# Which PSUM banks plain tiles, norm sums and the last mixer products use, and the order of the first down pair, in a fused FFN–mixer–FFN step

## The chip, the core and the metric

The kernel runs on one core of a Trainium2 chip. A core has five engines that work side by side and meet through semaphores: TensorE (PE; its weight loads are shown as PEld), VectorE (DVE), ScalarE (ACT), GpSimd (POOL) and SyncE (SP, which here only issues DMAs). TensorE writes its results into PSUM, eight banks of 512 fp32 values in each of 128 partitions; VectorE and ScalarE read them from there. The metric is the time of one execution in microseconds, and the median of several is compared.

## The reference

One step of a hybrid decoder trunk on 520 tokens (a prompt of 512 and 8 single tokens that go on from a state), model width 1024, FFN width 2816, all in fp32:

```python
h = h + 0.5 * swiglu(rms_norm(h, ffn1_norm), ffn1_w_gate, ffn1_w_up, ffn1_w_down)
m, ... = hybrid_mixer(rms_norm(h, mix_norm), ...)   # in-projection, pooling, conv, SSD scan, gate, out-projection
h = h + m
h = h + 0.5 * swiglu(rms_norm(h, ffn2_norm), ffn2_w_gate, ffn2_w_up, ffn2_w_down)
return rms_norm(h, final_norm), new pool, conv and ssm states
# swiglu(x, wg, wu, wd) = (silu(x @ wg) * (x @ wu)) @ wd
```

## The kernel before

Activations lie feature by token: 128 features on the partitions, 520 tokens along the free dimension, worked on as two halves of 260 (`HALVES`, `HB`). A product in fp32 is made from parts: each operand is split into a high part (fp32r) and the rest (`split`: ScalarE rounds the high part into `whi` or `shi`, VectorE subtracts for `wlo` or `slo`), and `mm3` (L121 to L126) issues three matmuls, high by high (L122), high by low (L125) and low by high (L126).

**FFN.** The 22 tiles of the FFN width are taken in chunks of 6, 6, 6 and 4. A gate tile and its up tile, by the two halves of the input features, make a 2 by 2 block product, which is done with seven smaller products instead of eight (`product`, p = 1 to 7). One of the sums, in the trace `A`, takes one PSUM bank, and the other two, `BE`, take a pair. The weights of the seven products are the raw ones (`whi_4a`, `whi_4b` for tile 4) and sums of them that VectorE builds (L346 to L348, then split into `shi_4c`/`slo_4c` and `shi_4d`/`slo_4d`). In between ScalarE copies a sum aside (`ac`, L380) before the next product adds to it. `gates` and `close` (L392 to L415) put the sums together, multiply by the norm's factor `r_f`, take Silu and multiply gate and up. The order for a tile is in `step`: close the tile before, then products 5, 6, 3, 7, 2; product 4 comes after the next tile's first one.

Before the first chunk is in its stride, some tiles are done another way: `plain` takes the unsplit fp32 weights (one matmul of two passes for each, L311), and `plain_out` (L314 to L325) reads them: L319 multiplies the gate half by `r_f`, L321 is Silu, L322 multiplies by `r_f` again, L324 multiplies by the up half. In FFN1 these are tiles 0 and 3, in FFN2 tile 0. `rstds` computes the norm's factor: a matmul with ones into a bank (`psr`, L168), Sqrt and reciprocal (L169, L170).

After each of the first three chunks come its down products, two output tiles at a time (`(c, 0)`, `(c, 2)`, `(c, 4)`, `(c, 6)`: names `A1d`, `BE1d` in FFN1 and `A2d`, `BE2d` in FFN2), again by seven products. Their activations are the outputs of pairs of tiles, sums and differences of which `g_split` builds and splits: `gx` and `go` are the first and second tile of a pair, `xd` (in the trace `gd`) the differences, `gt` the split parts (L264 high, L265 low). The last chunk's down (`down`, L462, in FFN1) is made tile by tile (`dn`): two tiles are begun with three of the four FFN tiles, as the last one's output comes late, and are then completed one after the other; VectorE adds each half to `h` (L478), and `after` makes the mixer's input from it.

**Mixer.** Stages in an order written by hand (plan strings) do the in-projection (`dt`, `inbc`, `inx`, `inz`), pooling, convolution, SSD scan, gate and out-projection (`wout`, three units; the last has `fin`, which makes FFN2's input from `h`). FFN2's tile 0 (`plain`) is laid between the last out-projection products by the plan `"h0 h2 h1 n0 h3 n1 n2 n3"`.

**PSUM in the FFNs** is one pool with three tags, two buffers each: `A` (one bank), `BE` (two banks) and `ps` (one bank): 2 + 4 + 2 banks. A tile that takes a buffer over waits until the readers of the one before are done. `bank(name)` gives a `ps` bank.

**What sets the order.** The program is written in order, and a scheduler then chooses each engine's instruction order by a simulation of its timeline; each engine runs its list in that order. `keep_in_program_order` (argument `pin` of `mm3`) holds an instruction at its place in the program's order; `high_priority` moves work ahead. So another buffer or pin can change the order of other engines' work too.

Of the kernel before, what the change touches and what calls it, by code (L numbers as in the profile page):

```python
# [61 lines left out]
def tile_trunk_step(ctx: ExitStack, tc: tile.TileContext, ins: dict, outs: dict):  # L62
# [9 lines left out]
    dr = ctx.enter_context(tc.tile_pool(name="dr", bufs=1, space=DRAM))  # L72
    ps = [None]

    def bank(name):
        return ps[0].tile([P, 512], F32, tag="ps", name=name)

    vx = act.tile([P, NVEC + KD * NT], F32, tag="h", name="h")
    vec = vx[:, :NVEC]
# [48 lines left out]
    def ws(w, k, m=P):  # L128
        return w[:, k * m : (k + 1) * m]
# [32 lines left out]
        nc.scalar.activation(out=sq, in_=h[:, d], func=AF.Square)  # L162
        nc.vector.tensor_tensor(out=nx[2], in0=nx[2], in1=sq, op=ALU.add)

    def rstd(r, acc, hs, width, name):
        ps = bank(f"psr_{name}")[:, : hs.stop - hs.start]
        for k, sq in enumerate(acc):
            nc.tensor.matmul(ps, ones, sq, start=k == 0, stop=k == len(acc) - 1)  # L168
        nc.scalar.activation(out=r[:, hs], in_=ps, func=AF.Sqrt, bias=eps, scale=1.0 / width)  # L169
        nc.vector.reciprocal(out=r[:, hs], in_=r[:, hs])  # L170

    def rstds(nx, name):
        for b, hs in enumerate(HALVES):
            rstd(nx[3], [nx[2][:, hs]], hs, D, f"{name}{b}")

# [28 lines left out]
    class Ffn:  # L204
# [42 lines left out]
        def g_split(self, f, late=None):  # L247
            role = self.role(f)
            if role == "plain" and late is not False:
                self.g_plain(f, self.out[f])  # L250
            if role != "second":
                return
            last = f == self.chunks[self.chunk[f]][-1]
            if not last and late is False:
                return
            gx, go = self.gx, self.out[f]
            if not last or late is not True:
                self.gt[f] = (self.gp.tile([P, 14, HB], F32R, tag="gt", bufs=3, name=f"gt{self.i}_{f}"),
                              self.gp.tile([P, 4, HB], F32, tag="xd", name=f"gd{self.i}_{f}"))
            t, xd = self.gt[f]  # L260

            def low(x, q):
                hi, lo = t[:, 0:7][:, q], t[:, 7:14][:, q]
                nc.scalar.copy(hi, x)  # L264
                nc.vector.tensor_tensor(out=lo, in0=x, in1=hi.bitcast(F32), op=ALU.subtract)  # L265

            if not last or late is not True:
                nc.vector.tensor_tensor(out=xd[:, 0], in0=gx[:, 0], in1=gx[:, 1], op=ALU.subtract)
                nc.vector.tensor_tensor(out=xd[:, 1], in0=go[:, 1], in1=gx[:, 1], op=ALU.subtract)
                nc.vector.scalar_tensor_tensor(out=xd[:, 2], in0=xd[:, 1], scalar=-1.0, in1=gx[:, 0], op0=ALU.mult,  # L270
                                               op1=ALU.subtract)
                low(gx[:, 0], 0)
                if last:
                    low(go[:, 1], 2)
                    low(xd[:, 0:3], slice(3, 6))
            if last and late is False:
                return
            nc.vector.scalar_tensor_tensor(out=xd[:, 3], in0=xd[:, 2], scalar=-1.0, in1=go[:, 0], op0=ALU.mult,
                                           op1=ALU.subtract)
            if last:  # L280
                low(go[:, 0], 1)
                low(xd[:, 3], 6)
            else:
                low(go, slice(1, 3))
                low(xd, slice(3, 7))
# [11 lines left out]
                nc.sync.dma_start(out=next(q), in_=next(q))  # L297

        def plain(self, f, xg, j, us=(0, 1)):
            for u in us:  # L300
                if (f, u) not in self.banks:
                    n = f"P{self.i}_{f}{u}"
                    if f and u == 0:
                        bs = [ps[0].tile([P, 512], F32, tag="A", bufs=2, name=f"{n}{b}") for b in range(2)]
                    else:
                        t = ps[0].tile([P, 2, 512], F32, tag="BE", bufs=2, name=n)
                        bs = [t[:, 0], t[:, 1]]
                    self.banks[f, u] = bs
                for q in range(2):
                    for b, slot in enumerate(((0, 1), (3, 2))):  # L310
                        nc.tensor.matmul(self.banks[f, u][b][:, :HB], ws(self.raw[f][:, u], j + 4 * q), xg[:, slot[q]],  # L311
                                         start=j == q == 0, stop=j == 3 and q == 1, skip_group_check=True)
# [42 lines left out]
        def product(self, k, p):  # L355
# [13 lines left out]
            for j in range(n):  # L369
                if isinstance(k, tuple):  # L370
                    t = self.gt[self.chunks[k[0]][2 * j + 1]][0]
                    xhi, xlo = t[:, slot], t[:, 7 + slot]
                else:
                    xhi, xlo = xth[:, j, slot], xtl[:, j, slot]
                mm3(out[:, :HB], ws(whi, k0 + j), ws(wlo, k0 + j), xhi, xlo, opens and j == 0,
                    j == n - 1, skip_group_check=True)
            a, c = self.ac[k]
            keep = {1: a[:, 0], 6: a[:, 1], 7: c[:, 0], 5: c[:, 1]}.get(p)
            if keep is not None:
# [82 lines left out]
        def down(self, c, lo, hi, after):  # L462
            n = hi - lo
            banks, units = {}, {}

            def part(d, ks):
                if d not in units:
                    units[d] = load_unit(ins[f"w{self.i}d"][d, :, lo * P : hi * P], n * P, f"{self.i}d{d}_{c}")
                    banks[d] = ps[0].tile([P, 2, 512], F32, tag="BE", bufs=2, name=f"dn{self.i}_{d}_{c}")
                wh, wl = units[d]  # L470
                for b in range(2):
                    for k in ks:
                        g = self.g[lo + k]
                        mm3(banks[d][:, b, :HB], ws(wh, k), ws(wl, k), g[:, 0, b], g[:, 1, b], k == 0, k == n - 1)

            def done(d):
                for b, hs in enumerate(HALVES):
                    nc.vector.tensor_tensor(out=h[:, d, hs], in0=banks[d][:, b, :HB], in1=h[:, d, hs], op=ALU.add)  # L478
# [12 lines left out]
        def down_by_half(self, c, lo, after, wd):  # L491
# [186 lines left out]
def mixer(tc, ins, outs, e):  # L678
# [556 lines left out]
```

## Time and profile before

| | us |
|---|---|
| median of 3 runs | 984.54 (983.57 to 985.28) |
| the profiled execution, as a whole | 984.47 |
| its span (what the trace covers) | 982.6 |
| PE busy in the span | 951.5 |
| DVE busy | 877.8 |
| ACT busy | 678.2 |

FFN1 runs from the start to about 361 us, the mixer to about 633, FFN2 to the end. In the views that follow, a timeline row gives start, duration (both us), engine, line, operation, output<-inputs, shape, the number of instructions that the row holds, and in brackets the engine's idle time before it and what ended it. A row of stages gives the stretch and its length, then for PE, PEld, DVE, ACT and POOL the busy time and the number of instructions, and last the granted TensorE clock, the DMA engines' busy share and GB/s. A row of waits gives engine, line and what was waited for, then the total, the count and the longest. Tile names in rows are without buffer numbers, except those of weights (`whi_1d_0a`: down weights, first pair, part a).

### The profile page before, as it was taken

The page shows a single profiled execution, that of the slowest core. Times are in us where ns is not written, and L with a number is a line of the kernel's source. Part 1 is how long each engine was busy: PE and PEld are TensorE (multiplying, and loading weights), DVE is VectorE, ACT ScalarE, POOL GpSimd, SP SyncE. Part 2 cuts the span into 40 slices and gives each one's busy share as a digit, 9 for nine tenths or more (in the row PEclk, how much of TensorE's full clock was granted, in tenths as well). Part 3 has the DMA queues.
Part 4 walks back from the last instruction along what each step waited for, and adds up shares of the span by engine and source line. Part 5 has one row for each costly group of instructions (what it writes and reads, how often), then busy time and mean ns, then how long its engine had stood idle before and what let it go on. Part 6 is the DMA issues. An engine that isn't in the chain of part 4 may idle for free.

```text
span 982.6 us, 20242 instructions
## 1 busy us (share of the span) xinstructions
PE 951.5 (97%) x7636; PEld 927.4 (94%) x7636; DVE 877.8 (89%) x1624; ACT 678.2 (69%) x1263; POOL 217.9 (22%) x319
## 2 busy tenths in 40 slices
PE   7999999999999999999999999999999999999995
PEld 6899999999999999999899998989999999999995
DVE  7899899989989698788979987999999999999976
ACT  7677677677777475685754335678788888888864
POOL 0112211121121000157411000113333233233300
PEclk9999999999999999999999999999999999999998
DMA  5565766576566243262335232456687768767732
GB/s 182 161 172 114 191 161 143 133 186 175 124 149 165 65 148 119 87 210 86 115 120 165 96 115 90 106 152 164 164 213 185 183 156 223 190 155 189 190 91 88
DMA packets 63571, 145.46 MB, mean 148 GB/s; under 512 B 9257, under 2 KB 22505, under 8 KB 63473
## 3 DMA queue, kind: packets, MB, share of 16 engines
q1 hardware_dynamic: 41168, 103.78, 33.2%
q0 software_dynamic: 22304, 40.38, 22.5%
q8 instruction: 60, 0.98, 0.4%
q14 instruction: 39, 0.31, 0.1%
HBM read 136.80 MB, written 7.34 MB: 147 GB/s over the span
## 4 chain that ended last, share of the span: by engine, by line
PE 85%; DVE 8%; ACT 3%; issue 2%; DMA 1%; POOL 1%; SPq 0%; DVEq 0%; ACTq 0%
PE A L126 7%; PE A L122 7%; PE A L125 7%; PE BE L122 6%; PE BE L125 6%; PE BE L126 6%; PE P L311 3%; PE wo L122 2%; PE wo L125 2%; PE wo L126 2%; PE inz L122 2%; PE A2d L125 2%; PE A2d L126 2%; PE A1d L125 2%; PE A1d L126 2%
## 5 line engine op out<-in xcount | busy, mean ns | idle before, releaser
L380 ACT COPY ac<-A 128x260 f32<-128x260 f32 x123 | 45.1, 369 | 16.8 <-PE A L126 16.5
L311 PE MATMUL P<-xg_f,raw 128*128 128x260 f32 x192 | 45.9, 398 | 5.5 <-DMA raw<-in_w1gu 5.5
L346 DVE TENSOR_TENSOR s<-raw 128x1024 f32<-128x1024 f32 x41 | 49.8, 1216 | 1.4 <-DMA raw<-in_w2gu 1.4
L311 PEld LDWEIGHTS P<-xg_f,raw 128*128 128x128 f32 x192 | 37.5, 199 | 11.5 <-ACT xg_f L188 5.4
L943 POOL DMA_DIRECT2D out_nss<-hs x32 | 20.6, 643 | 79.2 <-DVE hs L961 74.0
L106 ACT CAST whi_wo<-raw_wo 128x1024 fp32r<-128x1024 f32 x12 | 12.5, 1046 | 36.5 <-issue 9.2
L125 PE MATMUL wo<-catg,whi_wo 128*128 128x260 f32 x128 | 36.4, 285 | 1.3 <-DVE catg L1092 1.3
L122 PE MATMUL wo<-catg,whi_wo 128*128 128x260 f32 x128 | 37.3, 292 | 0.3 <-DVE h L1061 0.3
L122 PE MATMUL inz<-xh_mx,whi_inz 128*128 128x260 f32 x128 | 36.8, 288 | 0.0
L122 PE MATMUL inx<-xh_mx,whi_inx 128*128 128x260 f32 x128 | 36.4, 285 | 0.0
L126 PE MATMUL wo<-catg,wlo_wo 128*128 128x260 f32 x128 | 36.3, 284 | 0.0
L126 PE MATMUL inz<-xh_mx,wlo_inz 128*128 128x260 f32 x128 | 36.2, 283 | 0.0
L126 PE MATMUL inx<-xh_mx,wlo_inx 128*128 128x260 f32 x128 | 36.2, 283 | 0.0
L125 PE MATMUL inz<-xl_mx,whi_inz 128*128 128x260 f32 x128 | 36.2, 283 | 0.0
L125 PE MATMUL inx<-xl_mx,whi_inx 128*128 128x260 f32 x128 | 36.1, 282 | 0.0
L392 DVE TENSOR_TENSOR tg<-BE,ac 128x520 f32<-128x520 f32 x41 | 28.3, 691 | 5.2 <-PE BE L126 5.2
L807 DVE SCALAR_TENSOR_TENSOR A<-U,h,A 128x544 f32<-128x544 f32 x36 | 28.0, 778 | 4.3 <-ACT A L805 3.3
L401 DVE TENSOR_TENSOR tg<-tg,r_f 128x520 f32<-128x520 f32 x41 | 28.4, 694 | 1.3 <-ACT tg L399 1.0
L398 DVE TENSOR_TENSOR tg<-tg,r_f 128x520 f32<-128x520 f32 x41 | 28.4, 692 | 0.1
L347 DVE TENSOR_TENSOR s<-s,raw 128x512 f32<-128x512 f32 x41 | 28.0, 682 | 0.0
L348 DVE TENSOR_TENSOR s<-s,raw 128x512 f32<-128x512 f32 x41 | 27.9, 681 | 0.0
L399 ACT ACTIVATE tg<-tg 128x520 f32<-128x520 f32 x41 | 26.1, 637 | 1.0 <-DVE tg L398 0.9
(1787 smaller groups left out, 4747.4 us busy)
## 6 DMA issues: line engine op xcount, KB each, us to landing
raw<-in_w2gu SPq DMA_DIRECT2D x44, 512.0 KB, 4.9
raw<-in_w1gu SPq DMA_DIRECT2D x42, 512.0 KB, 4.7
raw_1d<-in_w1d SPq DMA_DIRECT2D x24, 384.0 KB, 4.0
raw_2d<-in_w2d SPq DMA_DIRECT2D x24, 384.0 KB, 4.0
raw_wo<-in_w_out SPq DMA_DIRECT2D x12, 512.0 KB, 4.8
ab<-scr_acs SPq DMA_DIRECT2D x8, 512.0 KB, 4.4
h<-in_state_ssm SPq DMA_DIRECT2D x16, 256.0 KB, 3.8
raw_inz<-in_w_in SPq DMA_DIRECT2D x8, 512.0 KB, 4.1
```

The lines of the kernel that those rows point to most:

```text
L122: first = nc.tensor.matmul(ps, whi, xhi, start=start, stop=False, **kw)
L125: nc.tensor.matmul(ps, whi, xlo, start=False, stop=False, **kw)
L126: nc.tensor.matmul(ps, wlo, xhi, start=False, stop=stop, **kw)
L311: nc.tensor.matmul(self.banks[f, u][b][:, :HB], ws(self.raw[f][:, u], j + 4 * q), xg[:, slot[q]], start=j == q == 0, stop=j == 3 and q == ...
L346: nc.vector.tensor_tensor(out=s1, in0=diag, in1=up0, op=ALU.add)
L347: nc.vector.tensor_tensor(out=s2[:, 0], in0=s1[:, 1], in1=raw[:, 0, :nb], op=ALU.add)
L348: nc.vector.tensor_tensor(out=s2[:, 1], in0=s2[:, 0], in1=raw[:, 0, nb : 2 * nb], op=ALU.add)
L380: nc.scalar.copy(keep, out[:, :HB])
L392: nc.vector.tensor_tensor(out=tg, in0=self.BE[k][:, :, :HB], in1=a, op=ALU.add)
L398: nc.vector.tensor_tensor(out=tg, in0=tg, in1=r, op=ALU.mult)
L401: nc.vector.tensor_tensor(out=tg, in0=tg, in1=r, op=ALU.mult)
L807: nc.vector.scalar_tensor_tensor(out=A[:, :n], in0=U[:, j : j + n], scalar=w(j), in1=A[:, :n], op0=ALU.mult, op1=ALU.add)
```

## The change

1. `bank` takes a tag. The up half (u = 1) of every plain tile goes into the two `ps` banks and the gate half into a `BE` pair. Before, tile 0 had both halves in `BE` pairs, and tile 3 its gate half in the two `A` banks and its up half in a `BE` pair.
2. The norm sums of the FFNs (`scales`) use `A` banks instead of `ps`.
3. The last out-projection products (`wout` with `fin`) use `A` banks instead of `ps`.
4. In `g_split` of a chunk's last pair the low parts of the differences `xd[:, 0:3]` are written ahead of those of `go[:, 1]`.
5. In the first down pair of a chunk (`(c, 0)`), the first matmul of each product is held in program order.
6. FFN1's last down begins three tiles with three of four FFN tiles instead of two; the third has its sums in the two `ps` banks.

```diff
-    def bank(name):
-        return ps[0].tile([P, 512], F32, tag="ps", name=name)
+    def bank(name, tag="ps"):
+        return ps[0].tile([P, 512], F32, tag=tag, name=name)
...
-    def rstd(r, acc, hs, width, name):
-        ps = bank(f"psr_{name}")[:, : hs.stop - hs.start]
+    def rstd(r, acc, hs, width, name, tag="ps"):
+        ps = bank(f"psr_{name}", tag)[:, : hs.stop - hs.start]
...
-    def rstds(nx, name):
+    def rstds(nx, name, tag="ps"):
         for b, hs in enumerate(HALVES):
-            rstd(nx[3], [nx[2][:, hs]], hs, D, f"{name}{b}")
+            rstd(nx[3], [nx[2][:, hs]], hs, D, f"{name}{b}", tag)
...
                 low(gx[:, 0], 0)
                 if last:
+                    low(xd[:, 0:3], slice(3, 6))
                     low(go[:, 1], 2)
-                    low(xd[:, 0:3], slice(3, 6))
...
         def plain(self, f, xg, j, us=(0, 1)):
-            for u in us:
+            for u in sorted(us, reverse=True):
                 if (f, u) not in self.banks:
                     n = f"P{self.i}_{f}{u}"
-                    if f and u == 0:
-                        bs = [ps[0].tile([P, 512], F32, tag="A", bufs=2, name=f"{n}{b}") for b in range(2)]
+                    if u:
+                        bs = [bank(f"{n}{b}") for b in range(2)]
                     else:
                         t = ps[0].tile([P, 2, 512], F32, tag="BE", bufs=2, name=n)
                         bs = [t[:, 0], t[:, 1]]
                     self.banks[f, u] = bs
+            for u in us:
...
                 mm3(out[:, :HB], ws(whi, k0 + j), ws(wlo, k0 + j), xhi, xlo, opens and j == 0,
-                    j == n - 1, skip_group_check=True)
+                    j == n - 1, pin=j == 0 and isinstance(k, tuple) and k[1] == 0, skip_group_check=True)
...
         def scales(self):
-            rstds(self.nx, f"f{self.i}")
+            rstds(self.nx, f"f{self.i}", "A")
...
-                    banks[d] = ps[0].tile([P, 2, 512], F32, tag="BE", bufs=2, name=f"dn{self.i}_{d}_{c}")
+                    if d == 2:
+                        banks[d] = [bank(f"dn{self.i}_{d}_{c}{b}") for b in range(2)]
+                    else:
+                        t = ps[0].tile([P, 2, 512], F32, tag="BE", bufs=2, name=f"dn{self.i}_{d}_{c}")
+                        banks[d] = [t[:, 0], t[:, 1]]
...
-            part(0, range(n - 1))
-            part(1, range(n - 1))
-            part(0, range(n - 1, n))
-            done(0)
-            part(1, range(n - 1, n))
-            done(1)
-            for d in range(2, KD):
-                part(d, range(n))
+            for d in range(3):
+                part(d, range(n - 1))
+            for d in range(KD):
+                part(d, range(n - 1, n) if d < 3 else range(n))
                 done(d)
...
-                ps = bank(f"wo{j}_{d}{b}")
+                ps = bank(f"wo{j}_{d}{b}", "ps" if fin is None else "A")
```

More of the change, by code (lines that the diff above doesn't have):

```diff
@@ L473, in part @@
                         g = self.g[lo + k]
-                        mm3(banks[d][:, b, :HB], ws(wh, k), ws(wl, k), g[:, 0, b], g[:, 1, b], k == 0, k == n - 1)
+                        mm3(banks[d][b][:, :HB], ws(wh, k), ws(wl, k), g[:, 0, b], g[:, 1, b], k == 0, k == n - 1)
             def done(d):
                 for b, hs in enumerate(HALVES):
-                    nc.vector.tensor_tensor(out=h[:, d, hs], in0=banks[d][:, b, :HB], in1=h[:, d, hs], op=ALU.add)
+                    nc.vector.tensor_tensor(out=h[:, d, hs], in0=banks[d][b][:, :HB], in1=h[:, d, hs], op=ALU.add)
                     after(d, b, hs)
-            part(0, range(n - 1))
-            part(1, range(n - 1))
-            part(0, range(n - 1, n))
-            done(0)
-            part(1, range(n - 1, n))
-            done(1)
-            for d in range(2, KD):
-                part(d, range(n))
+            for d in range(3):
+                part(d, range(n - 1))
+            for d in range(KD):
+                part(d, range(n - 1, n) if d < 3 else range(n))
                 done(d)
```

## The prediction

> **What bounds the kernel now.** I read the page's busy shares and chain first, then the busy time by stage, then the list of what TensorE waited for, then the timeline round each wait that the change can touch.
>
> ```profile
> PE 951.5 (97%) x7636; PEld 927.4 (94%) x7636; DVE 877.8 (89%) x1624; ACT 678.2 (69%) x1263; POOL 217.9 (22%) x319
> PE 85%; DVE 8%; ACT 3%; issue 2%; DMA 1%; POOL 1%; SPq 0%; DVEq 0%; ACTq 0%
> ```
>
> TensorE is busy for 951.5 of 982.6 us, so only 31.1 us of idle are there for any reordering to win, and VectorE (DVE) at 89% is the next in line. By stage (length, busy PE, PEld, DVE, ACT, POOL):
>
> ```profile
> 61.00:340.00 279.00, 276.60 (x2289) 274.92 (x2287) 251.79 (x412) 196.20 (x347) 49.53 (x59) 1.00 0.62 148
> 340.00:368.00 28.00, 26.25 (x212) 25.28 (x213) 24.91 (x58) 20.30 (x44) 0.70 (x2) 1.00 0.38 130
> 600.00:661.00 61.00, 58.56 (x423) 55.60 (x422) 52.37 (x81) 41.98 (x69) 7.98 (x11) 1.00 0.42 115
> ```
>
> In the steady FFN (61 to 340) TensorE is idle for 2.4 of 279 us. A microsecond lost ahead of it is therefore not made up in it, and one gained is kept only if VectorE, 90% busy there, keeps up. The edits act at four places: the start of FFN1 (25 to 61), the passage from each chunk's last product to its down pairs, FFN1's last down (339 to 366), and the passage from the mixer to FFN2 (600 to 661). The waits that belong to these, and the longest of any (total, times, longest):
>
> ```profile
> PE BE2d L125 <- DVE gt L265: 1.7, 2, 0.9
> PE dt L737 <- DVE dt_v L757: 1.4, 1, 1.4
> PE BE L122 <- ACT ac L380: 1.6, 3, 1.0
> PE psr_y L168 <- ACT X L1083: 1.6, 1, 1.6
> PE A L122 <- ACT ac L380: 1.4, 3, 0.5
> PE BE1d L125 <- DVE gt L265: 0.8, 3, 0.3
> ```
>
> **The change, part by part.** No instruction is added or removed on any engine. What changes is which PSUM bank a result lies in, hence which read a matmul must wait for, and the order that the scheduler writes, which I read from the two programs.
>
> *Plain tiles at the start of FFN1.* Before, in time order (start, duration):
>
> ```profile
> 29.04 0.70 DVE L319 TENSOR_TENSOR tg<-P,r_f 128x260 f32<-128x260 f32 x2
> 29.66 0.68 DVE L113 TENSOR_TENSOR wlo_1a<-raw,whi_1a 128x512 fp32r<-128x512 f32 x1
> 29.79 6.87 PEld L311 LDWEIGHTS P<-xg_f,raw 128*128 128x128 f32 x32 [0.22 <-DVE tg L319]
> 31.16 1.28 ACT L321 ACT_TABLE_LOAD   x1
> 32.99 1.03 ACT L106 CAST shi_1c<-s 128x1024 fp32r<-128x1024 f32 x1
> 34.34 1.22 DVE L113 TENSOR_TENSOR slo_1c<-s,shi_1c 128x1024 fp32r<-128x1024 f32 x1
> 35.47 0.76 DVE L324 SCALAR_TENSOR_TENSOR gx<-P,tg 128x260 f32<-128x260 f32 x2
> 36.72 0.47 PE L122 MATMUL A<-xth_f,whi_1a 128*128 128x260 f32 x1
> 39.80 0.28 PE L122 MATMUL A<-xth_f,shi_1d 128*128 128x260 f32 x1
> 42.15 0.39 PE L122 MATMUL A<-xth_f,whi_4a 128*128 128x260 f32 x1 [0.76 <-ACT whi_4a L106]
> 42.94 0.39 PE L122 MATMUL BE<-xth_f,shi_1d 128*128 128x260 f32 x1 [0.29 <-ACT ac L380]
> 48.57 0.28 PE L122 MATMUL BE<-xth_f,shi_4c 128*128 128x260 f32 x1
> ```
>
> The up half of tile 3 (16 fp32 matmuls of two passes, 29.79 to 36.7, 6.9 us) waits 0.22 us for L319, which reads P_0's gate half out of its BE tile. That work fills PE while ScalarE loads its table, does the Silu and splits the next weights. In the changed kernel both up halves use the two "ps" banks, so tile 3's up half must wait for the last reader of tile 0's: L324, 35.47 to about 36.23, 7 us later, because it stands behind Silu and L322. The scheduler puts the 12 matmuls A<-whi_1a and the 12 BE<-shi_1c ahead of it, and these wait too. A matmul's pitch is 0.12 us (46 from 42.94 to 48.57). A<-1a goes from 29.8 to 31.5, held a little by wlo_1a (30.34). BE<-1c needs shi_1c (34.02) and at its third matmul slo_1c (35.56): idle about 2.5 and 1.3 us. It ends at 36.8, and tile 3's up half then runs to 43.8, where before the same work was done at 39.80: +4.0. From there 60 matmuls (A<-1d, BE<-1d, BE<-1a, A<-1c, A<-4a) bring it to 51.05; before, that point was 48.57. The two stalls at 42.15 and 42.94 (0.76 and 0.29 idle, with late starts and the longer first matmuls 1.6) are gone, as their weights are now long ready. So **+2.5 us**. VectorE gets tile 3's result about 4 us later; by the durations above slo_4d then comes at about 54.3, when PE wants it at 54.4. That fits barely, so the range is +2 to +4.
>
> *Pinned down pair and the swap in g_split.* Before, at the first of the boundaries:
>
> ```profile
> 91.24 0.97 DVE L265 TENSOR_TENSOR gt<-gd,gt 128x780 fp32r<-128x780 f32 x1
> 91.70 0.28 PE L122 MATMUL A1d<-gt,shi_1d_0d 128*128 128x260 f32 x1
> 92.26 0.39 PE L125 MATMUL BE1d<-gt,shi_1d_0c 128*128 128x260 f32 x1 [0.28 <-DVE gt L265]
> 92.86 0.38 ACT L380 COPY ac1d<-BE1d 128x260 f32<-128x260 f32 x1 [0.37 <-PE BE1d L126]
> 93.29 0.39 PE L122 MATMUL BE1d<-gt,shi_1d_0d 128*128 128x260 f32 x1 [0.28 <-ACT ac1d L380]
> ```
>
> Two short waits stand there: on the low parts of the last pair (L265 of 780 elements, ready 92.21), then on the copy of BE1d (93.24). The first sets PE back by 0.44 us (92.26 less 91.70 less one pitch), and the matmul after a wait takes 0.39 in place of 0.28, 0.11 more; the second costs as much. The pins put all nine BE1d<-c matmuls ahead of A1d<-d, so PE reaches the one that needs L265 seven matmuls (0.84 us) earlier and waits longer; the nine A1d<-d then stand between BE1d's end and BE1d<-d and cover the copy. They start at 92.6 and end at 93.7, where before BE1d<-d started at 93.29: +0.4, less 0.11 for a restart saved, **+0.3**. The swap in g_split should bring L265(780) forward, but the list of VectorE's instructions has the same ones before it as before. That gives +0.3 at 92, 184 and 276, and also at 796 and 889 (the two BE2d waits); the pair at 704 waits for a copy only and I take 0. Sum **+1.5 us** (−1 to +2).
>
> *Three partial tiles in FFN1's last down.*
>
> ```profile
> 339.36 0.51 PE L122 MATMUL dn<-gt,whi_1d 128*128 128x260 f32 x2 [0.58 <-ACT gt L244]
> 340.14 0.39 PE L125 MATMUL dn<-gt,whi_1d 128*128 128x260 f32 x1 [0.28 <-DVE gt L245]
> 341.05 1.43 DVE L478 TENSOR_TENSOR h<-dn,h 128x260 f32<-128x260 f32 x4 [0.96 <-PE dn L126]
> 341.87 0.39 PE L122 MATMUL dn<-gt,whi_1d 128*128 128x260 f32 x1 [0.26 <-DVE h L478]
> 360.74 0.29 PE L737 MATMUL dt<-xh_mx,w 128*48 128x260 f32 x1 [1.35 <-DVE dt_v L757]
> 365.23 0.47 PE L122 MATMUL inbc<-xh_mx,whi_inbc 128*128 128x260 f32 x1
> ```
>
> The third tile's partial fills 339.4 to 341.9, where three waits (0.58, 0.28, 0.26 idle, with their restarts about 1.9 us) stand now, and the hand-over at 360.74 (1.5 us with its restart) goes because dt's bank is no longer dn_7's. But dn_0's end, and with it L478, comes 1.2 us later, and VectorE is 24.9 of 28 us busy from 340: its queue from L478 on ends in the norm and the xl parts that the in-projection at 365.23 waits for. PE's gain turns into waiting there. **−0.2 us** (−1.5 to +0.5).
>
> *Norm sums and last mixer products in the A banks, plain tile of FFN2.*
>
> ```profile
> 644.48 0.70 DVE L322 TENSOR_TENSOR tg<-tg,r_f 128x520 f32<-128x520 f32 x1 [1.23 <-ACT tg L321]
> 646.75 0.39 PE L122 MATMUL BE<-xth_f,shi_3d 128*128 128x260 f32 x1 [1.02 <-ACT ac L380]
> 650.26 1.22 DVE L113 TENSOR_TENSOR slo_1d<-s,shi_1d 128x1024 fp32r<-128x1024 f32 x1
> 660.06 0.29 PE L122 MATMUL A<-xth_f,whi_1b 128*128 128x260 f32 x1
> ```
>
> With P_0's up half in "ps" one BE tile is free, so tile 3's BE products come between its A products and cover the copies: the waits of A on ac (1.4 us and their restarts) and the 1.02 us at 646.75 go, and PE is some 2.5 us ahead at about 649. Then it needs slo_1d, ready at 651.48 before. In the changed order VectorE does tile 3's L392 and L398 and wlo_4a ahead of it; the step it is moved past costs 0.6 us each, the wait at 644.48 shrinks, and slo_1d comes at about 652. PE stands for some 3 us, and the 68 matmuls after it end at about 660.1, against 660.06: **0** (−2.8 to +1).
>
> **Sum.** 984.47 us is the profiled execution (span 982.6 and 1.87 us around it), 0.07 under the median of the runs. 984.47 + 2.5 + 1.5 − 0.2 + 0 = **988.3 us**. About 0.2%, 2.0 us, can be told from no change.
>
> **Rivals.** *Faster:* the swap makes L265(780) earlier in time although not in the list, and both boundary waits go. At 92, 184 and 276 these are worth about 1.1 us each (0.44 + 0.11 twice); at 796 and 889, where the first wait is 0.9 and not 0.3, 1.7. That is 6.7 us instead of a loss of 1.5: 984.47 + 2.5 − 6.7 − 0.2 = 980.1. It decides from the point where L265 ends 1.2 us earlier against PE than now. For it: PE's later arrival, if VectorE isn't late as well. Against: VectorE's unchanged list. *Nothing to measure:* the 2.8 us of the mixer's end are kept, because VectorE has the parts of tile 1 ready sooner than I count: 988.3 − 2.8 = 985.5. For it the 1.23 us that VectorE idles at 644.48; against it three operations put ahead of slo_1d. *The change doesn't do what it says:* the scheduler leaves the boundaries as they are; then only the FFN1 start counts, about 986.8. *Slower still, the clock:*
>
> ```profile
> L311 PE MATMUL P<-xg_f,raw 128*128 128x260 f32 x11 | 5.0, 644 | 5.5 <-DMA raw<-in_w1gu 5.5
> L311 PE MATMUL P<-xg_f,raw 128*128 128x260 f32 x20 | 4.5, 382 | 0.0
> ```
>
> These are PE's groups from 6 to 10 and from 12 to 16 us (count | busy, mean ns | idle before): after the idle first 5.5 us 11 such passes run in 4 us, later 20, so a start from idle costs about 2 us. If a gap of 2.5 us, or 2.5 and 1.3 with two matmuls between, is enough to bring that back, FFN1's start costs 2 more and the mixer's end, with its 3 us, perhaps 2 as well: 990.3 to 992.3. The longest wait inside the run before is 1.6 us (psr_y above), and no row shows it there. [...]
>
> **How the numbers follow.** Forecast (988.3, own range 986.5 to 991): 0.50. Boundaries gain: 0.15, and with the mixer's gain as well (977.3) 0.05. Mixer's gain kept: 0.13. Boundaries unchanged: 0.07. Clock: 0.10. The range leaves out the far end of the gains and the second clock loss: 980 to 991.5. Faster by over 0.2% (under 982.5): the 0.20 and a little of the mixer case, 0.22. Within: 0.20. Slower (over 986.5): 0.58.
>
> **What would show it.** In the profile after: tile 3's up half starting at about 36.8, with a wait of PE on shi_1c and slo_1c before it, and BE<-shi_4c at about 51.0; at the boundaries one wait on L265 of over 1 us and none on ac1d; no wait at dt; a wait of about 3 us on slo_1d near 650. I am wrong if BE<-shi_4c starts before 50, if the wait on L265 is under 0.4 us, or if the stretch from the in-projection to FFN2's A<-whi_1b (365.23 to 660.06) gets over 1 us shorter.

## The result

| | median of the runs (lowest to highest) | ratio to before, 95% interval |
|---|---|---|
| before | 984.71 us (983.57 to 985.68, 6 runs) | |
| after | 990.01 us (988.47 to 991.47, 6 runs) | 1.0055 (1.0042 to 1.0069) |

The changed kernel is slower by 0.55%, 5.3 us between the medians, where 3.8 us were forecast. Its profiled execution took 991.27 us (span 989.5). The page, busy shares and chain of the kernel after:

```profile
PE 955.6 (97%) x7636; PEld 930.5 (94%) x7636; DVE 877.7 (89%) x1624; ACT 679.4 (69%) x1263; POOL 217.9 (22%) x319
PE 81%; DVE 11%; ACT 3%; issue 2%; POOL 2%; DMA 0%; SPq 0%; DVEq 0%; ACTq 0%
```

VectorE does the same work in the same time. TensorE, with the same 7636 matmuls, is busy for 4.1 us more, and idle for 33.9 us in place of 31.1. Same matmuls in more busy time is the first sign that some of them ran slower. The list of TensorE's waits after (total, times, longest):

```profile
PE BE2d L125 <- DVE gt L265: 2.9, 2, 1.5
PE BE1d L125 <- DVE gt L265: 2.6, 3, 0.9
PE A L126 <- DVE wlo_1a L113: 1.4, 1, 1.4
PE A L122 <- ACT shi_1d L106: 1.3, 1, 1.3
PE dt L737 <- DVE xl_mx L144: 1.2, 1, 1.2
PE A L126 <- DVE slo_1d L113: 1.2, 1, 1.2
PE BE L122 <- ACT shi_1c L106: 1.0, 1, 1.0
PE BE L126 <- DVE slo_1c L113: 0.9, 1, 0.9
PE BE L122 <- ACT ac L381: 0.5, 2, 0.3
```

The waits on `ac` (3.0 us before) have shrunk to 0.5, those on `ac1d` are gone from the list, and the copy's place is taken by longer waits on L265 (2.5 before, 5.5 now) and by five waits on freshly split weights at the two FFN starts.

Where the time went is read off the starts of TensorE's landmarks in the two timelines (us between the first matmuls of the names given; the last two columns are kernels of the experiments below):

| stretch | before | after | e4, FFN1's homes back | e11, gaps filled |
|---|---|---|---|---|
| start to psr_f | 24.56 | 23.50 | 23.64 | 24.64 |
| FFN1 start: psr_f to BE<-shi_4c | 24.01 | 28.77 | 23.94 | 26.62 |
| FFN1 with its three boundaries, to dn | 281.40 | 282.34 | 282.38 | 282.34 |
| last down: dn to inbc | 35.26 | 34.95 | 34.99 | 34.98 |
| mixer: inbc to psr_y | 176.76 | 176.81 | 176.35 | 177.79 |
| FFN2 start: psr_y to A<-whi_1b | 118.07 | 119.90 | 119.08 | 118.39 |
| FFN2 with its boundaries, to psl | 304.95 | 305.59 | 306.17 | 305.67 |
| psl to the end | 17.62 | 17.64 | 17.64 | 17.63 |
| span | 982.63 | 989.50 | 984.19 | 988.06 |

Two stretches hold nearly all of it: FFN1's start, +4.8, and FFN2's start, +1.8. The first, in TensorE's timeline after:

```profile
28.88 0.28 PE L125 MATMUL A<-xtl_f,whi_1a 128*128 128x260 f32 x1
30.51 0.39 PE L126 MATMUL A<-xth_f,wlo_1a 128*128 128x260 f32 x1 [1.35 <-DVE wlo_1a L113]
31.69 0.28 PE L126 MATMUL A<-xth_f,wlo_1a 128*128 128x260 f32 x1
32.95 0.58 PE L122 MATMUL BE<-xth_f,shi_1c 128*128 128x260 f32 x1 [0.99 <-ACT shi_1c L106]
33.34 0.42 PE L125 MATMUL BE<-xtl_f,shi_1c 128*128 128x260 f32 x1
34.66 0.58 PE L126 MATMUL BE<-xth_f,slo_1c 128*128 128x260 f32 x1 [0.90 <-DVE slo_1c L113]
36.78 0.42 PE L126 MATMUL BE<-xth_f,slo_1c 128*128 128x260 f32 x1
36.99 8.23 PE L312 MATMUL P<-xg_f,raw 128*128 128x260 f32 x32
44.87 0.47 PE L122 MATMUL A<-xth_f,shi_1d 128*128 128x260 f32 x1
52.27 0.28 PE L122 MATMUL BE<-xth_f,shi_4c 128*128 128x260 f32 x1
```

The order and the waits are the forecast ones: A<-whi_1a, then BE<-shi_1c held by `shi_1c` and `slo_1c`, then tile 3's up half, at 36.99 where 36.8 was forecast. But from 32.95 a matmul lasts 0.42 us instead of 0.28, and the 32 passes that follow take 7.9 us to the next group instead of 6.9 before. The windows say why. Before, then after (busy PE, PEld, DVE, ACT, POOL; then the granted clock, DMA share, GB/s):

```profile
28.50:37.00 8.50, 8.50 (x40) 7.22 (x39) 7.53 (x14) 6.03 (x8) 1.83 (x2) 1.00 0.44 77
654.00:662.00 8.00, 8.00 (x69) 8.00 (x68) 7.86 (x13) 7.06 (x15) 0.87 (x1) 1.00 0.66 179
```

```profile
28.50:37.00 8.50, 5.26 (x27) 4.49 (x27) 8.00 (x15) 6.23 (x9) 1.84 (x2) 0.72 0.42 63
37.00:45.00 8.00, 8.00 (x34) 6.75 (x33) 4.60 (x6) 1.95 (x3) 0.85 (x1) 0.87 0.56 163
654.00:662.00 8.00, 6.31 (x37) 6.11 (x38) 6.57 (x13) 3.18 (x6) 2.34 (x4) 0.79 0.82 203
```

The granted clock falls to 0.72 in the stretch of the waits, is still 0.87 after it, and falls again to 0.79 at FFN2's start. Over the whole span it was 0.991 in this run and 0.994 to 0.996 in the other five, against 0.996 to 0.997 in every run of the kernel before but a single one, of 1333 us at 0.751, which no comparison here uses.

These shares are means. In the traces of before and after the record itself has two values, 1.00 and 0.50. After's stands at 0.50 for 6.83 us from 32.30 and for 3.41 us from 656.94, and these two falls lie 183 times 3.41 us apart. Cut at steps of this length, each of the two follows a step in which TensorE had little work, 1.73 and 1.25 of 3.41 us:

```profile
28.89:32.30 3.41, 1.73 (x13) 1.31 (x11) 3.41 (x8) 3.38 (x6) 1.84 (x2) 1.00 0.40 63
32.30:39.13 6.83, 5.27 (x17) 4.50 (x18) 5.42 (x8) 2.84 (x5) 0.00 (x0) 0.50 0.60 145
653.53:656.94 3.41, 1.25 (x8) 1.05 (x9) 3.41 (x5) 1.70 (x3) 2.56 (x4) 1.00 0.98 261
656.94:660.35 3.41, 3.41 (x18) 3.41 (x17) 3.04 (x8) 0.90 (x2) 0.00 (x0) 0.50 1.03 237
```

### The profile page after: what moved, and what is told of

Same layout as the page of the kernel before. It is cut to its first block, busy times and chain, and to the rows that moved or that the text cites. A ratio compares the mean times of both kernels' runs of the same rounds, so it can differ in the third digit from the quotient of the medians.

```text
span 989.5 us, 20246 instructions
## 1 busy us (share of the span) xinstructions
PE 955.6 (97%) x7636; PEld 930.5 (94%) x7636; DVE 877.7 (89%) x1624; ACT 679.4 (69%) x1263; POOL 217.9 (22%) x319
## 4 chain that ended last, share of the span: by engine, by line
PE 81%; DVE 11%; ACT 3%; issue 2%; POOL 2%; DMA 0%; SPq 0%; DVEq 0%; ACTq 0%
PE A L122 8%; PE A L126 8%; PE A L125 8%; PE BE L122 6%; PE BE L126 6%; PE BE L125 6%; PE P L312 2%; PE wo L122 2%; PE wo L126 2%; PE wo L125 2%; PE A1d L125 2%; PE A1d L122 2%; PE A1d L126 2%; PE inz L122 2%; PE inz L126 2%
## 5 line engine op out<-in xcount | busy, mean ns | idle before, releaser
L122 PE MATMUL inz<-xh_mx,whi_inz 128*128 128x260 f32 x128 | 36.8, 287 | 0.1
```

What stands on the lines that cost most here:

```text
L122: first = nc.tensor.matmul(ps, whi, xhi, start=start, stop=False, **kw)
```

## The experiments

The question was first which edit carries the loss, then how much of it is waiting and how much the clock, and last whether the boundaries can be gained. Ratios are to the kernel before on the same chip in the same rounds, with 95% intervals. The groups e1 to e4, e5 to e8, e9 with e10, and e11 with e12 ran on four chips, and no run of after is on record beside them, so ratios are to be compared and not medians.

| kernel | median, us | ratio | granted clock of the runs |
|---|---|---|---|
| e1, edits 1 to 3 alone | 989.33 | 1.0040 (1.0025 to 1.0056) | 0.991 to 0.995 |
| e2, edits 4 and 5 alone | 986.01 | 1.0010 (1.0001 to 1.0019) | 0.996 to 0.997 |
| e3, edit 6 alone | 984.67 | 0.9997 (0.9987 to 1.0007) | 0.996 to 0.997 |
| e4, after with FFN1's homes of before | 986.55 | 1.0015 (1.0005 to 1.0025) | 0.993 to 0.997 |
| e5, after, 22 matmuls in FFN1's gap | 992.34 | 1.0079 (1.0060 to 1.0099) | 0.992 to 0.997 |
| e6, after, 18 in FFN2's gap | 991.02 | 1.0066 (1.0053 to 1.0080) | 0.991 to 0.996 |
| e7, both | 991.51 | 1.0077 (1.0060 to 1.0093) | 0.993 to 0.996 |
| e9, 12 + 22 + 18 | 990.40 | 1.0069 (1.0057 to 1.0082) | 0.994 to 0.997 |
| e11, 12 + 22 + 10 | 989.65 | 1.0063 (1.0051 to 1.0075) | 0.996 in all five |
| e8, e3 with a warm-up at the start | 984.17 | 0.9998 (0.9989 to 1.0006) | 0.995 to 0.997 |
| e10, e3 with the low parts split | 982.39 | 0.9981 (0.9972 to 0.9990) | 0.996 to 0.997 |
| e12, e10 with a warm-up | 984.47 | 1.0009 (0.9999 to 1.0019) | 0.993 to 0.997 |

**e1: the PSUM homes alone** (edits 1 to 3 on the kernel before).

```diff
+            for u in sorted(us, reverse=True):
...
+                    if u:
+                        bs = [bank(f"{n}{b}") for b in range(2)]
...
+            rstds(self.nx, f"f{self.i}", "A")
...
+                ps = bank(f"wo{j}_{d}{b}", "ps" if fin is None else "A")
```

> The kernel before with edits 1 to 3 alone (plain tiles, norm sums and last mixer products in their new banks). My theory, places that add up, read from the trace after: the start of FFN1 costs 3.7 us and the passage to FFN2 1.5 to 1.8, part of both from a lower TensorE clock, so 988.5 to 990.5 with a clock in the records under 0.996 in most runs, and waits on wlo_1a, shi_1c, slo_1c, shi_1d and slo_1d. Rival, the loss comes from the pinned down pair shifting VectorE's order: within 1 us of before.

The homes carry most of the loss: 1.0040. The waits of e1 at both FFN starts are those of after:

```profile
PE BE L122 <- ACT shi_1c L106: 1.9, 1, 1.9
PE A L122 <- ACT shi_1d L106: 1.3, 1, 1.3
PE A L126 <- DVE slo_1d L113: 1.2, 1, 1.2
PE BE L126 <- DVE slo_1c L113: 1.0, 1, 1.0
```

From psr_f to BE<-shi_4c its profiled run takes 29.2 us, and its clock is 0.991 to 0.995.

**e2: the pinned down pair and the swap.**

```diff
+                    low(xd[:, 0:3], slice(3, 6))
                     low(go[:, 1], 2)
-                    low(xd[:, 0:3], slice(3, 6))
...
+                    j == n - 1, pin=j == 0 and isinstance(k, tuple) and k[1] == 0, skip_group_check=True)
```

> The kernel before with edits 4 and 5 alone (order in g_split, pinned first down pair). My theory: 0.3 us lost at each of five boundaries, 986.2 (1.5 us more than before), one wait on L265 of about 0.9 us in FFN1 and 1.5 in FFN2 in place of two. Rival, the pins cover the copies of ac1d and pay: 0.5 us a boundary less, 982.

1.0010, so the rival in which the boundaries gain 6.7 us is out. The two rows of L265 in its list of waits are word for word those of after (2.9, 2, 1.5 and 2.6, 3, 0.9), and FFN1's three boundaries take 0.32 us more than before each, on the mean. The swap was not run by itself: with it or without it each engine gets its instructions in the same order in the built program, of before as of after, so edit 4 changes nothing.

**e3: three partial tiles in the last down.**

```diff
+                    if d == 2:
+                        banks[d] = [bank(f"dn{self.i}_{d}_{c}{b}") for b in range(2)]
...
+            for d in range(3):
+                part(d, range(n - 1))
+            for d in range(KD):
+                part(d, range(n - 1, n) if d < 3 else range(n))
```

> The kernel before with edit 6 alone (three partial tiles in FFN1's last down). My theory: the waits at 339 to 342 go and come back at dt, where VectorE's xl parts are awaited: 0.3 us less than before (0.8 less to 0.2 more). Rival, the 1.9 us filled are kept: 982.8.

0.9997: nothing that can be told. The stretch from dn to inbc is 0.3 us shorter (34.98). The hand-over at the first `dt` matmul goes, as forecast (it starts 28.6 us after dn, for 30.8 before), and ahead of a later one stands a wait for VectorE's xl parts:

```profile
PE dt L736 <- DVE xl_mx L144: 1.2, 1, 1.2
```

What edit 6 is worth depends on the other edits, though. In e1, which has the new homes without it, the hand-over is gone too, there is no wait at `dt`, and the stretch takes 34.00 us, 0.95 less than in after. In the changed kernel edit 6 so seems to lose about 0.9 us where by itself it gains 0.3; no run takes it alone out of after, so this is read from e1.

**e4: after, with FFN1's plain tiles and norm sums in the banks of before.**

```diff
+            for u in (us if self.i == 1 else sorted(us, reverse=True)):
...
+                    if self.i == 1 and f and u == 0:
+                        bs = [bank(f"{n}{b}", "A") for b in range(2)]
+                    elif self.i == 2 and u:
+                        bs = [bank(f"{n}{b}") for b in range(2)]
...
+            rstds(self.nx, f"f{self.i}", "ps" if self.i == 1 else "A")
```

> The changed kernel with FFN1's plain tiles and norm sums in the banks of before. My theory: FFN1's start is as before, so 3.7 us less than the changed kernel in a run like the profiled one, 986.5 to 987.5. Rival, the gap's cost is covered by later waits: within 1 us of the changed kernel, 989 to 990.5.

The ratio goes back from 1.0055 to 1.0015, about 3.9 us, and FFN1's start takes 23.94 us as before (the table of stretches). FFN1's homes are therefore the main term. Of the 0.0015 that is left, e2 has 0.0010. The clock of the ten runs beside the profiled one is still 0.993 to 0.995: of the two places, FFN2's start is left in it. In the profiled run (0.997) the clock did not fall there, although TensorE has the same two waits as in after, of 1.3 us on `shi_1d` and 1.2 on `slo_1d`. The steps of the clock record, counted back from its fall at 977.76 us, lie otherwise there, so that each of them holds one of the two waits:

```profile
646.67:650.08 3.41, 2.13 (x16) 1.74 (x14) 3.41 (x8) 3.34 (x6) 2.07 (x4) 1.00 0.75 202
650.08:653.49 3.41, 2.19 (x19) 2.16 (x19) 3.41 (x7) 0.30 (x2) 1.12 (x3) 1.00 1.00 202
```

**e5, e6, e7: is it the waiting or the clock?** Matmuls of no use for the result (into a bank that is overwritten right after) stand where TensorE waits, so that it is busy through the gap.

```diff
+FILL = ((1, 5, 22, 0),)                  # e5; e6: ((2, 6, 18, 0),); e7: both
...
+            for i, at, m, dd in FILL:
+                if (self.i, k, p) == (i, 1, at):
+                    for _ in range(m):
+                        f = nc.tensor.matmul(self.BE[k][:, dd, :HB], ws(self.w[k][1][0][0], 0), xth[:, 0, 0],
+                                             start=True, stop=False, skip_group_check=True)
+                        tc.keep_in_program_order(f)
```

> The changed kernel with 22 more matmuls, of no use for the result, between A<-whi_1a and BE<-shi_1c at the start of FFN1; every other instruction is in the same order. They take 2.6 us of PE where it now waits 1.0 us for shi_1c and 0.9 us for slo_1c. Clock theory: the clock falls there because PE does too little for some microseconds; kept busy it doesn't fall, the 12 BE<-shi_1c run at a pitch of 0.12 us and tile 3's up half in 7.0 us and not 8.2. That saves 2.4 us and the fill costs 0 to 0.5: 2 us less than the changed kernel, 988, and FFN1's clock at 1. Rival, the slow matmuls there come from something else (PSUM banks shared with VectorE's reads, weights loaded late): the fill then only costs, 990 to 992.5.

> The changed kernel with 18 more matmuls, of no use for the result, ahead of A<-shi_1d at the start of FFN2, where PE waits 1.3 and 1.2 us for shi_1d and slo_1d; the rest in the same order. Clock theory: 20 matmuls after this wait run at a pitch of 0.2 us and not 0.12, which the fill keeps away: 1.7 us less than the changed kernel, 988.3. Rival: VectorE sets the pace there (slo_4c, slo_4d), so the faster matmuls wait again a few microseconds later: within 0.5 us of the changed kernel.

> The changed kernel with both fills. Clock theory: 3 to 4 us less than the changed kernel, 986 to 987, with a spread from run to run as small as that of the kernel before (2 us) and a mean clock of 0.997. What is then left over the kernel before is the waiting alone: 1.3 us at FFN1's start and 1.5 us at the boundaries, less 0.3. Rival (the clock is an effect and not the cause): 990 or more.

In the profiled runs the fills do what the clock theory says of their place: psr_f to BE<-shi_4c is 25.9 us in e5 and 26.4 in e7, against 28.8 in after, 29.2 in e1 and 29.1 in e6, which leaves FFN1's gap open. But the medians (1.0066 to 1.0079) are not under after's, and the runs spread over up to 7 us with clocks of 0.991 to 0.997. As a proof by time these three fail. The gap for `wlo_1a` was still open (0.5 us in e5's profile, 1.35 in after's). The fill at FFN2's start costs time of its own: that stretch is 119.0 us in e6 and 119.1 in e7, and 118.39 in e5, which has no fill there and whose clock did not fall there either. And the clock can fall elsewhere: e7's profile has its one fall in the mixer, at 480.88 us, with a mixer of 179.6 us for after's 176.8.

**e9, e11: all the gaps, no longer than they are.**

```diff
+FILL = ((1, 1, 12, 0), (1, 5, 22, 0), (2, 6, 18, 0))      # e9
+FILL = ((1, 1, 12, 0), (1, 5, 22, 0), (2, 6, 10, 0))      # e11
```

The 12 matmuls of both, and the 10 of e11, are not held in program order; the other fills are.

> The changed kernel with matmuls of no use for the result in each gap of FFN1's start: 12 where PE waits for wlo_1a, 22 where it waits for shi_1c and slo_1c, and the 18 of FFN2's start as before. What the run with 22 alone left open: its profiled run showed full clock and 2.7 us gained there, but its other runs were slow and had a mean clock of 0.992 to 0.996. Clock theory, refined: the clock falls where PE's share of work over a window of some microseconds is low, and where that window lies changes from run to run; the gap for wlo_1a, left open, was enough in most runs. With no gap left the FFN1 part can't lose its clock in any run: mean clock 0.996 or more in at least 5 of 6, 987.5 to 989.5. Rival, the fills themselves cost and the clock isn't a matter of gaps: 991 or more, clock 0.992 to 0.995 as with the other fills.

> The changed kernel with FFN1's two fills (12 and 22) and only 10 in FFN2's start, which then fit into the gap for slo_1d (the 18 outlasted it by 0.8 us in the trace). Clock theory: what is left is the waiting that the new order makes, without the clock's loss: 2.5 us at FFN1's start, 1.5 at the boundaries, 0.3 at FFN2's start, less 0.3: 4.0 us over the kernel before, ratio 1.004, clock 0.996 to 0.997, and runs closer together than the changed kernel's 3 us. Rival, the fills cost time by themselves also where they fit into a gap: ratio 1.0065 or more, as with the other fills.

In e11 the two fills of FFN1, TensorE's timeline, and the same windows as above:

```profile
30.14 1.70 PE L374 MATMUL BE<-xth_f,whi_1a 128*128 128x260 f32 x12
32.88 2.81 PE L374 MATMUL BE<-xth_f,whi_1a 128*128 128x260 f32 x22
```

```profile
28.50:37.00 8.50, 8.50 (x66) 8.26 (x65) 7.77 (x14) 6.36 (x9) 1.84 (x2) 1.00 0.41 77
37.00:45.00 8.00, 8.00 (x43) 7.06 (x42) 4.54 (x6) 3.40 (x5) 0.85 (x1) 1.00 0.43 140
654.00:662.00 8.00, 7.51 (x60) 7.30 (x61) 8.00 (x15) 4.51 (x9) 2.40 (x5) 1.00 0.80 205
```

The clock is 1.00 in all of them, and all five runs have 0.996, where after's go down to 0.991. They lie within 0.8 us and after's six within 3.0; that the clock makes the difference is not shown, since the kernel before spreads over 2.1 to 4.1 us in its rounds at an even clock. At FFN1's start the clock fell in all three profiles with the gaps open (after, e1, e6) and in none of the four with fills (e5, e7, e9, e11). e9, whose last fill is 8 matmuls longer than its gap, takes 119.14 us at FFN2's start for e11's 118.39, and one of its five runs still has 0.994. FFN1's start is 26.62 us, FFN2's 118.39: without the drop the waiting costs 2.6 and 0.3 us. The expected ratio was missed, though: 1.0063, not under after's 1.0055. So by time the fills have not been shown to gain. The table of stretches shows where it went in the profiled runs: 3.7 us are won at the two starts; 1.1 is lost before psr_f, where after was early (23.50, with 23.6 to 25.5 in the other profiles), and 1.0 in the mixer. The latter has a cause of its own. The DMA view of after from 407 to 410 us, then of e11 from 406 to 409 (issue, count, KB, us from issue to landing):

```profile
scr_dt<-dts SPq DMA_DIRECT2D x1, 0.5 KB, 1.3
```

```profile
q8 instruction: 1, 0.02, 2.1%
scr_dt<-dts SPq DMA_DIRECT2D x1, 0.5 KB, 1.8
```

In e11 a packet of the queue that the view calls `q8 instruction`, of 0.02 MB, takes 1.0 us just then (2.1% of 16 engines in 3 us), and the small write, which VectorE's `sdt` waits for, lands 0.5 us later. VectorE's timeline, after and e11:

```profile
415.59 0.23 DVE L887 TENSOR_TENSOR sdec<-sdt,aexp 128x64 f32<-128x64 f32 x1 [3.10 <-DMA sdt<-scr_dt]
426.63 1.43 DVE L1004 TENSOR_SCALAR ab<-ab,tok 128x128 f32<-128x128 f32 x1 [1.87 <-POOL we L991]
```

```profile
415.10 0.23 DVE L895 TENSOR_TENSOR sdec<-sdt,aexp 128x64 f32<-128x64 f32 x1 [3.59 <-DMA sdt<-scr_dt]
426.78 1.42 DVE L1012 TENSOR_SCALAR ab<-ab,tok 128x128 f32<-128x128 f32 x1 [2.54 <-POOL we L999]
```

VectorE waits 0.5 and then 0.7 us longer, and TensorE then 0.9 us on `catp` (L863), a wait that after does not have. In the traces of all six kernels with additional matmuls ahead of the mixer (e5, e7, e8, e9, e11, e12) a packet of this queue starts within 0.5 us of the write's issue, and the write takes 1.7 to 2.8 us; in the other eight the next one starts 2.6 us or more after it, and the write takes 1.3. The mixer of the six takes 177.6 to 179.6 us, that of the eight 176.1 to 176.8. That the packet is the cause is read from this coincidence; no run moved it by itself.

**e8, e12: the other way round, a warm-up at the start.** Square fp32 matmuls of `ones` while the first loads are under way: 16 in e8 on top of e3, 10 in e12 on top of e10.

```diff
+                    if (self.i, f, u) == (1, 0, 0):
+                        for _ in range(16):
+                            nc.tensor.matmul(bs[0][:, :P], ones, ones, start=True, stop=False, skip_group_check=True)
```

> The kernel before with edit 6 and 16 matmuls of ones by ones, of no use for the result, in the first microseconds, where PE waits 5.5 us for the first weights. Clock theory: the first passes of the plain tiles then take 0.22 us from the start and not 0.43 for 4.9 us, and the kernel gains what of these 2.4 us later work doesn't wait for: 982.5 to 984. Rival: the input loads set the pace until 25 us, so the start of FFN1's products stays where it is: 984.5.

> The kernel before with edit 6, the split low part, and 10 matmuls of ones by ones ahead of the first plain tile. With 16 the trace showed the plain tiles at 0.22 us a pass from the first one on, but they began 2 us late, at 7.5. Ten take 4.1 us and end at 5.2, when the first weights are there. Clock theory: 1 to 2 us less than with the split alone, ratio 0.9965 to 0.997. Rival, VectorE and ScalarE, which prepare the inputs, set the pace until 25 us: ratio 0.998 as without.

TensorE's groups of e8 from 6 to 10 us:

```profile
L314 PE MATMUL P<-xg_f,raw 128*128 128x260 f32 x12 | 2.8, 383 | 0.0
```

The plain passes last 383 ns from their first on, against 644 from 6 to 10 us before and 382 from 12 to 16, but the warm-up itself takes 0.20 us for a pass of 128 columns (32 in 6.6 us), about as long as before's passes of 260 take from 12 to 16 us (20 in 4.5 us), and ends at 7.5 us, 2.0 after the loads had come: gain and delay cancel, 0.9998. e12 missed: its mixer is 1.4 us longer than before's, with the packet just described, and it has two waits that e10 does not have, 1.8 us on `tg` (L323) in FFN1 and 1.4 on `slo_2d_0d` in FFN2.

**e10: can the boundary wait be removed?** On e3: the first third of `xd`'s low parts, which the next down product needs, is written by itself ahead of the rest, so that L265's 780 elements become 260 and 520.

```diff
+                    low(xd[:, 0], 3)
                     low(go[:, 1], 2)
-                    low(xd[:, 0:3], slice(3, 6))
+                    low(xd[:, 1:3], slice(4, 6))
```

> The kernel before with edit 6, and in g_split of a chunk's last pair the low part of the first difference split off as an operation of its own ahead of the others, in place of the one of 780 elements. My theory on the boundaries: the wait is on VectorE's position of that one operation, and not on TensorE's order, so giving BE1d's third triple its part early removes the wait on L265 and, as A1d and BE1d are then mixed, the wait on the copy: 1.1 us less at each of three boundaries and up to 1.7 at two, less 0.2 each for the longer VectorE work: 979 to 982. Rival, VectorE sets the pace at the boundary in any order: 984 to 985.

982.39 us, 0.9981 (0.9972 to 0.9990): faster than both kernels, but less than expected: the kernel before had 983.65 us in these rounds, so the gain is 1.3 us by the medians and 1.9 by the ratio, and the 979 to 982 stood for 2.5 to 5.5. The waits on L265 and on `ac1d` and `ac2d`, 4.7 us in e3, are gone from the list, and in their place stand 4.0 us of others:

```profile
PE BE2d L122 <- ACT shi_2d_1c L106: 1.4, 1, 1.4
PE BE2d L122 <- ACT shi_2d_2c L106: 1.4, 1, 1.4
PE A1d L122 <- DVE gx L408: 1.2, 3, 0.4
```

TensorE comes to the next products earlier than their weights and inputs; most of the gain is given back there.

## Why the prediction was right or wrong

**FFN1's start, +2.5 forecast: right as a wait, too small as a time.** Order and releasers were as said: the waits on `shi_1c` and `slo_1c`, and the third, on `wlo_1a`, 1.35 us where the forecast had it "held a little". That tile 3's up half starts at 36.99 for 36.8 is partly luck: after's psr_f came 1.06 us earlier than before's, and the halved clock took as much back. Counted from psr_f, 12.2 us were forecast, and it is 13.5 in after and 12.4 in e11, whose clock did not fall. Without a clock drop the stretch costs +2.6 (e11; +1.9 in e5). With the drop, as in after, e1 and e6, it costs 4.8 to 5.2. BE<-shi_4c at 52.27 instead of 51.0 is that difference less an earlier psr_f.

**The clock, put at nothing in the sum and given as a rival with 0.10: this is the step that failed.** The price, 2 us a place, was about right: 2.15 us at FFN1's start and 1.5 at FFN2's (after less e11). What was wrong is the condition. That gaps of 2.5 and 1.3 us at FFN1's start and of 3 us at FFN2's leave the clock alone, as the sum has it, was the author's estimate, which no run shows; the rival's own wording, two gaps with two matmuls between, was nearer to what happened. At FFN1's start after has waits of 1.35, 0.99 and 0.90 us, and the clock fell all the same: from 28.57 to 34.66 us only 14 matmuls start, where 50 would fit at the pitch of 0.12 us. The longest idle of TensorE in this trace between 6 and 970 us, 1.56 us ahead of `psr_y` at 583.41, was followed by no fall. So the length of a single gap does not tell here whether the clock fell; TensorE's busy time within one step of the record does, in the two traces of before and after. From 10 us on (the record begins at 10.2 us in before and at 8.4 in after) they have four falls, the last of each in its last 9 us, and these follow steps in which TensorE was busy for 0.28 (before, 972.80 to 976.22), 1.73, 1.25 and 1.78 us (after, 977.79 to 981.20). The least busy of the other steps at full clock has 1.85 us in both, and it is the one with the wait ahead of `psr_y` (576.86 to 580.27 and 581.85 to 585.26).

Whether it falls varies from run to run (0.991 to 0.996). That the steps lie elsewhere in each run is an estimate, from e4's profiled run, where they did. In e2, e3, e10 and e11 the runs are all at 0.996 or 0.997. In e4, e5, e9 and e12 the profiled run is at 0.996 or 0.997 too, but others go down to 0.992 to 0.994. So the gaps at FFN2's start, which e4 has as after has them, cost time only in some runs, and what sets the clock of a run without a trace is not shown.

After's lowest run, 988.47 us at 0.996, is the one nearest to 988.3. From it to the median, 1.5 us, is what the clock costs in a typical run: an estimate, since only one run has a trace, and the times do not confirm it. e11 less its 1.0 us in the mixer would be at about 1.0053, which cannot be told from after's 1.0055.

**Boundaries, +0.3 each: right for the five, wrong for the sixth.** In FFN1 +0.31 in after, +0.32 in e2, one wait on L265 in place of two short ones. At the first, TensorE's timeline after:

```profile
94.75 0.28 PE L122 MATMUL BE1d<-gt,shi_1d_0c 128*128 128x260 f32 x1
95.92 0.38 PE L125 MATMUL BE1d<-gt,shi_1d_0c 128*128 128x260 f32 x1 [0.89 <-DVE gt L265]
96.26 0.28 PE L122 MATMUL A1d<-gt,shi_1d_0d 128*128 128x260 f32 x1
```

The wait sets TensorE back by 1.05 us (95.92 less 94.75 less one pitch), 0.89 of it idle, where "over 1 us" was named (the two in FFN2 are 1.5). The two in FFN2 cost 0.29 and 0.33, so the five together are 1.6 for 1.5. The pair at 704, put at 0, costs as well: from FFN2's first matmul with `shi_6d` to its first with `whi_9b` it is 50.86 us before, 51.17 in after and 51.68 in e2, with a wait of 0.4 us on `slo_2d_0d` that before does not have. In after this +0.31 is hidden, as the work ahead of it takes 0.30 less. That the swap is empty held, and the rival built on it fell with e2.

**Last down, −0.2: right in size and nearly in place.** It is −0.3. The hand-over at the first `dt` matmul went, and the gain turned into a wait for VectorE's xl parts, as the step said, only 1.4 us ahead of the in-projection, at the last `dt` matmuls, and not at it:

```profile
368.12 0.29 PE L737 MATMUL dt<-xl_mx,w 128*16 128x260 f32 x1 [1.25 <-DVE xl_mx L144]
```

What the step did not see is that the new homes alone remove the hand-over (e1, 34.00 us), and that edit 6 then costs more than it gains.

**FFN2's start, 0: right but for the clock.** The waits of TensorE on the copies go, and those on the split weights come, two of 1.3 and 1.2 us (`shi_1d`, `slo_1d`) instead of one of 3:

```profile
654.47 0.39 PE L122 MATMUL A<-xth_f,shi_1d 128*128 128x260 f32 x1 [1.27 <-ACT shi_1d L106]
656.47 0.39 PE L126 MATMUL A<-xth_f,slo_1d 128*128 128x260 f32 x1 [1.22 <-DVE slo_1d L113]
```

Without the drop the stretch is +0.3 (e11 and e5) or +1.0 (e4, with two more waits, of 0.5 and 0.3 us, on `slo_4c` and `slo_4d`), with it +1.8 (after and e1). The rival that keeps the mixer's 2.8 us is out in both cases.

Put together without the drop: 0.1 at the first loads, 2.6, 0.9, −0.3, 0.3 and 0.7 in e11 less its mixer add up to 4.4 us (unrounded) against the forecast 3.8, 984.47 + 4.4 = 988.9. The forecast for the waits was good to 0.6 us. In after's profiled run the clock adds 3.7 us to such a sum, and the earlier psr_f takes 1.1 off.

## What to carry to other kernels

Giving a result another bank chooses which earlier reader a matmul must wait for (here tile 3's up half starts at 36.99 us and not at 29.79); ask what the scheduler will then put ahead of it, and whether that work's inputs are ready. Where several short waits come together, price them by TensorE's work in the whole stretch, and not by the longest of them: in the trace after, 3.41 us with 1.73 us of TensorE's work in them, round a wait of 1.35 us, were followed by a granted clock of 0.50, and 3.41 us with 1.85, round one of 1.56, were not. At FFN1's start the clock cost nearly as much again as the waits (2.15 us on 2.6). What an edit is worth by itself need not be what it is worth beside others (the third partial tile: −0.3 us alone, about +0.9 with the new homes). In e10 the waits that the down products had on one operation of VectorE and on the copies (4.7 us) went away when the part that was needed was written by itself; look next at what TensorE then reaches too early, here 4.0 us of other waits.

## What the runs showed of the hardware

Three waits of 1.35, 0.99 and 0.90 us within 6 us brought the granted clock to 0.72 over 28.5 to 37 us, and matmuls of 128x260 from 0.28 to 0.42 us; with 34 additional matmuls in the same gaps (e11) it stayed 1.00. In the traces of before and after the record has 1.00 and 0.50 alone. Cut at steps of 3.41 us from their falls, the two traces have four steps at full clock that a halved one followed, with 0.28, 1.25, 1.73 and 1.78 us of TensorE's work, and no other step at full clock with less than 1.85. At the kernel's start the warm-up of e8 brought the plain passes of 6 to 10 us from 644 to 383 ns.

Where a packet of the queue `q8 instruction` (0.02 MB) started within 0.5 us of a 0.5 KB write's issue, the write took 1.7 to 2.8 us and not 1.3, and the mixer behind it was 0.7 us or more longer than in any other kernel. Where the packet falls moved with additional matmuls ahead of it, and not with e6's behind it (5.5 us after the write's issue, 4.9 in after), so here an edit far away brought it on or not. That the packet is what delays the write is read from the coincidence alone.

Open remains why e5, e6 and e7 spread more than after, and why e5 has runs at 0.992.
